# A hybrid decoder step on one core: TensorE's order up to the first FFN pair written out as a table, with planner constants moved

## The chip, the cores and the metric

The kernel runs on one core of one Trainium2 chip. The metric is the device time of one execution in microseconds (us). Engines are named as in the profile: PE is TensorE, DVE is VectorE, ACT is ScalarE, POOL is GpSimd, SP is SyncE (here it only issues DMAs).

## The reference, cut to what matters

One layer for 2048 prompt tokens and 8 single-token samples, width 1024, all in float32:

```python
xn = _rmsnorm(x, norm1_g)
z = jnp.einsum('btd,de->bte', xn, w_in)
xr, gr, q, k, v = jnp.split(z, IN_SPLITS, axis=-1)
xc, new_conv = _causal_conv(xr, conv_buf, conv_w, conv_b)
hs, h_last = _rglru(xc, h0, gate_a_w, gate_a_b, gate_x_w, gate_x_b, lru_lambda)
rec = hs * jax.nn.gelu(gr)
att = sliding-window attention over self + 128 tokens, 8 heads on 2 KV heads, sinks
mix = jnp.concatenate([_rmsnorm(rec, rec_norm_g), _rmsnorm(att, attn_norm_g)], axis=-1)
h = x + jnp.einsum('bte,ed->btd', mix, w_out)
hn = _rmsnorm(h, norm2_g)
ff = jax.nn.silu(hn @ w_gate) * (hn @ w_up)
y = h + ff @ w_down
```

followed by a final RMSNorm. The FFN is 2816 wide.

## The kernel before, in words

Activations lie with channels on the 128 partitions and tokens along the free axis. A float32 product is made of three fp32r matmuls, weight high times input high, high times low, and low times high (`mm3` in the projections, the three calls in `products` and `down` in the FFN).

**The first stage** works on four blocks of tokens (520, then 3 × 512), block `s`. For each: load and norm (`xn{s}_{k}`, k of 8 channel chunks), the input projection in 14 column units (`ip{s}_{u}_{i}`, PSUM tiles of 260 or 512 tokens), convolution (`xc`), the two gates (`g{s}_{c}_{gi}`: one small matmul each, ACT's tanh to `ra` and `ia`), the scan, and attention in 16 blocks of 128 tokens: scores `s{b}_{kv}`, exponentials `sc`, four transposes `pt{b}_{kv}_{kb}`, ACT's `pth` and DVE's `ptl` (high and low part), output `o{b}_{kv}` and its scale `ratt`. Mean squares go through PE too: `st_*` sums over partitions, DVE and POOL turn the sum into 1/root (`cols`), `bc_*` spreads it over the partitions, and ACT copies it to a tile `rb_*`. The output projection `op{s}_{m}` has 8 units `m`. The last block's (`out_half`) is cut into halves: `op3_m_0` over the recurrent channels is added to the residual at once; `op3_m_1` over the attention channels is multiplied on DVE by `rb_at3` (L941), which comes from `bc_at3_0`, and then added to `xres3_m` (L942), which ACT's queue stores to `hs`.

**The FFN** runs over three groups of tokens of two halves each (344 or 342), and over 11 pairs of 128-wide chunks of the 2816. In a pair, 2 × 2 blocks are multiplied with seven products, in the order 1, 2, 6, 5, 7, 3, 4 (`g{group}_{pair}_{r}` for gate, `u...` for up, 12 matmuls each), with sums of weights `s1` to `s4` made on POOL, high parts of weights `w_g.._r` cast on ACT and low parts made on DVE or POOL. Product 1 is copied out of PSUM by ACT to `c_g0_0_10` (L1236) before product 6 continues in the same bank. The inputs of the products are tiles `hn0_*`: four loads `m0_r_kk` for each of seven mixed inputs from DRAM, through four staging tiles, each split into a high part on ACT (L432) and a low part on DVE (L433). The down products are `d{group}_{pair}_{m}_{half}` (tile names `pd`).

**What sets the order.** Each piece of work is a generator; the class `Chains` keeps them in a heap by due time, and a generator yields the time at which its next part is due, from constants: `T_IP` and `T_OP` for the projections of the four blocks, `T_OPA` for the second halves of the last output projection, `T_B0` for the start of the FFN, `F_HN` for the leads of the `hn` loads, `T_ATT`, `T_REC`, `D_ATT` and `D_REC` for attention and recurrence, and leads `L_*` by which single operations go ahead. The due time becomes the priority of what is emitted, and a list scheduler puts each engine's instructions in order by priority and by what is ready in its own model of time. PSUM is eight banks: three for projections and products (`acc_tile`), two for scores, one each for transposes, for attention outputs and for the small tiles (`m_tile`: gates, `st`, `bc`, `hb`, `vt`).

Of the kernel before, what the change touches and what calls it, by code (L numbers as in the profile page):

```python
# [12 lines left out]
P = 128  # L13
# [42 lines left out]
F_HN = [26.25, 18.3, 31.9]  # L56
# [44 lines left out]
T_B, T_END, T_PROD, T_DOWN, T_ROUND = plan()  # L101
O_KF = [8, 9, 10, 11, 12, 13, 0, 4, 1, 5, 2, 6, 3, 7]
# [6 lines left out]
T_REC = 46.56  # L109
L_PE, L_EV, L_DMA, L_W, L_PREP, D_PREP, L_AN, T_HN, D_HN, D_MIX = 195.07, 6.8, 44.07, 6.54, 16.82, -0.58, 33.49, 477.25, 7.78, 0.2  # L110
# [3 lines left out]
L_SW = 10.68  # L114
T_CACHE, T_LD, T_PRO = 126.26, 3.73, -37.62
D_REC = [10.95, 7.47]
D_ATT = [4.5, 3.07, 9.75, 5.73]
T_DVE = -4.47
T_DEC = 102.0
T_RN = [128.93, 254.29, 363.658, 427.88]  # L120
# [70 lines left out]
def hybrid_step(tc, xT, xR, vecs, cst, gatew, win, wout, wgate, wup, wdown, kT, vC, ck, cv, sconv, sh0,  # L191
# [4 lines left out]
    with ExitStack() as ctx:  # L196
# [81 lines left out]
        def mm3(out, ws, k, xh, xl, first, last):  # L278
# [3 lines left out]
            nc.tensor.matmul(out, wh, xl, start=False, stop=False)  # L282
            nc.tensor.matmul(out, wl, xh, start=False, stop=last)  # L283
# [16 lines left out]
        def rstd_cols(acc, w, nt, which, out, name, lead=None, pin=False):  # L300
            ps = m_tile(f"st_{name}")
            with ahead(lead):
                for j in range(nt):
                    r = nc.tensor.matmul(ps[:w, j:j + 1], acc[:, j * w:(j + 1) * w], avg[:, which:which + 1],
                                         start=True, stop=True)
                    if pin and j == 0:
                        keep(r)
            nc.vector.tensor_scalar(out, ps[:w, :nt], EPS, None, ALU.add)
            nc.gpsimd.tensor_tensor(out, out, nhalf[:w, :nt], op=ALU.pow)

        def row_bcast(cols, w, nt, name, lead=None, keep_ps=False, pin=False):
            out = None if keep_ps else bcp.tile([P, TM], F32, tag="bc", name=f"rb_{name}")
            per = 512 // w
            for j0 in range(0, nt, per):
                jn = min(per, nt - j0)
                ps = (acc_tile if keep_ps else m_tile)(f"bc_{name}_{j0}")
                with ahead(lead):
                    for j in range(jn):
                        r = nc.tensor.matmul(ps[:, j * w:(j + 1) * w], cols[:, j0 + j:j0 + j + 1].to_broadcast([w, P]),
                                             ident[:w, :w], start=True, stop=True)  # L320
# [4 lines left out]
                nc.scalar.copy(out[:, j0 * w:(j0 + jn) * w], ps[:, :jn * w])  # L325
            return out
# [7 lines left out]
        def half_bcast(gi, n, name):  # L334
# [3 lines left out]
            for s, (c0, T, _, w, nt) in enumerate(SUBS):  # L338
# [4 lines left out]
                with ahead():  # L343
                    for j in range(j0, j1):
                        x, y = max(a, c0 + j * w), min(b, c0 + j * w + w)
                        d0 = x - c0 - j * w
                        nc.tensor.matmul(ps[:, x - o:y - o], rs2[:w, s, j:j + 1].to_broadcast([w, P]),
                                         ident[:w, d0:d0 + y - x], start=True, stop=True)
# [91 lines left out]
        with ExitStack() as actx:  # L440
# [114 lines left out]
            def unit(s, u, dst, key=None):  # L555
# [7 lines left out]
                for i, (n0, nn) in enumerate(nbl):  # L563
                    ps = (first_tiles.pop(0) if first_tiles else acc_tile)(f"ip{s}_{u}_{i}")
                    for k in range(KD):
                        mm3(ps[:, :nn], w, k, xn[k][:, 0, n0:n0 + nn], xn[k][:, 1, n0:n0 + nn], k == 0, k == KD - 1)
# [10 lines left out]
            def rec_chunk(s, c):  # L577
# [26 lines left out]
                for gi, (dst, hb) in enumerate(((ra, hab), (ia, hxb))):  # L604
                    for n0, nn in nbl:
                        ps = m_tile(f"g{s}_{c}_{gi}_{n0}")
                        with ahead():
                            nc.tensor.matmul(ps[:, :nn], gw[:, (gi * 4 + c) * P:(gi * 4 + c + 1) * P], xc[:, n0:n0 + nn],
# [104 lines left out]
            def v_chunk(s):  # L713
                vr = ap2.tile([P, TM], F32, tag="xres", name=f"vraw{s}")
                yield from unit(s, 9, vr, ("k", s))
                for b in range(4):
                    yield ip_time(s, 9) + U_IP + b
                    ps = m_tile(f"vt{s}_{b}")
                    with ahead():
                        nc.tensor.transpose(ps[:, 0:P], vr[:, b * P:(b + 1) * P], ident)  # L720
# [19 lines left out]
            def attn_item(s, b, kv, t):  # L740
# [19 lines left out]
                for g2 in range(2):  # L760
                    ps = s_tile(f"s{gb}_{kv}_{g2}")
                    for gi in range(2):
# [21 lines left out]
                for i, kb in enumerate(kbs):  # L784
                    yield t + D_ATT[2] + i
                    pt = t_tile(f"pt{gb}_{kv}_{kb}")
                    with ahead():
                        for g in range(G):
                            nc.tensor.transpose(pt[:, g * P:(g + 1) * P], sc[:, g, i * P:(i + 1) * P], ident)
# [7 lines left out]
                for i, (kb, ph, pl) in enumerate(pts):  # L797
                    vt = vts[gb - 1 + kb][:, 2 * kv:2 * kv + 2, :].rearrange("p a d -> p (a d)")
                    with ahead():
                        nc.tensor.matmul(po, vt, ph, start=i == 0, stop=False)  # L800
                        nc.tensor.matmul(po, vt, pl, start=False, stop=i == len(pts) - 1)
# [6 lines left out]
            def decode(t):  # L808
# [17 lines left out]
                for b in range(NB):  # L826
                    nc.tensor.matmul(ps[:, b * 8:b * 8 + 8], kc[:, b * P:(b + 1) * P], qf[:, b * 8:b * 8 + 8],
# [7 lines left out]
                nc.tensor.transpose(ps2[0:64, 0:P], st, ident)  # L835
                nc.tensor.matmul(ps2[0:64, P:P + 1], w1[:, 128:192], ones[:, 0:1],
# [17 lines left out]
                nc.tensor.transpose(ps3[:, 0:64], sd[:, 0:P], ident[0:64, 0:64])  # L854
                nc.tensor.matmul(ps3[:, 64:128], ones[0:64, :], dg, start=True, stop=True)
# [3 lines left out]
                for b in range(NB):  # L859
                    nc.tensor.matmul(ps4[:, b * 8:b * 8 + 8], vc[:, b * P:(b + 1) * P], pt[:, b * 8:b * 8 + 8],  # L860
# [10 lines left out]
                nc.tensor.transpose(ps5[0:NB, 0:P], kvn[:, 0, :], ident)  # L871
                nc.tensor.transpose(ps5[0:NB, P:2 * P], kvn[:, 1, :], ident)
# [6 lines left out]
            def out_unit(s, m):  # L879
# [27 lines left out]
            def out_half(s, m, i):  # L907
# [75 lines left out]
        with ExitStack() as bctx:  # L983
# [181 lines left out]
            def products(gi, p, x):  # L1165
# [52 lines left out]
                for i, r in enumerate(PRODS):  # L1218
# [7 lines left out]
                    for kk in range(4):  # L1226
# [4 lines left out]
                        nc.tensor.matmul(ps, wh, hi, start=first, stop=False, skip_group_check=not fresh)  # L1231
                        nc.tensor.matmul(ps, wh, lo, start=False, stop=False, skip_group_check=not fresh)  # L1232
                        nc.tensor.matmul(ps, wl, hi, start=False, stop=kk == 3, skip_group_check=not fresh)  # L1233
# [20 lines left out]
            def down(gi, p):  # L1254
# [6 lines left out]
                for i, (m, n) in enumerate(order):  # L1261
                    yield t + U_D * i / 16, ("d", gi, p, 0, m // 4), ("d", gi, p, 1, m // 4)
                    ps = ps_tile(f"pd{gi}_{p}_{m}_{n}")[:, :nn]
                    for h in range(2):
# [3 lines left out]
                        nc.tensor.matmul(ps, w[:, 0, c:c + P], hi, start=h == 0, stop=False)  # L1268
                        nc.tensor.matmul(ps, w[:, 0, c:c + P], lo, start=False, stop=False)  # L1269
                        nc.tensor.matmul(ps, w[:, 1, c:c + P], hi, start=False, stop=h == 1)  # L1270
# [8 lines left out]
            def down_parts(gi, p):  # L1279
                nn = HALVES[gi][0][1]  # L1280
                acc = {}
                for n in range(14):
# [6 lines left out]
                    for j in range(2):  # L1289
# [73 lines left out]
            ch.run()  # L1363

# [100 lines left out]
```

## Time and profile before

| what | value |
|---|---|
| median of 3 runs | 2086.74 us (2085.59 to 2092.28) |
| profiled execution | 2083.33 us |
| its span, first to last instruction | 2081.6 us |
| mean granted PE clock | 0.988 |
| PE busy | 2020.7 us, 97% |
| first matmul | 8.10 us |
| start of the FFN's third product (`g0_0_6`) | 697.81 us |

The profile is of one execution. In a timeline row stand start, duration, engine, line of the kernel, operation, output and inputs by name without numbers, and how many equal instructions the row holds; in brackets the idle time ahead of it and what ended that. A row of a stretch gives its limits, its length, the busy time of PE, PEld (weight loads), DVE, ACT and POOL with the number of instructions, PE's granted clock, the DMA engines' busy share and GB/s.

### The profile page before, as it was taken

What the parts mean: (1) busy time and instruction counts of PE and PEld (TensorE: products, weight loads), DVE (VectorE), ACT (ScalarE), POOL (GpSimd) and SP (SyncE); (2) the same over time, 40 slices, a digit from 0 to 9 for tenths busy, and PEclk for the clock granted to TensorE, in tenths of its full rate; (3) what the DMA queues carried; (4) which work ended last, traced back from release to release, by engine and by line L of the source; (5) the groups of instructions that cost most, each with busy time, mean ns of one, the idle gap of its engine ahead of it and who ended that gap; (6) DMA issues with size and microseconds to landing.
All of it is one profiled execution on the core that took longest, in us unless ns stands there. A gap on an engine that the chain in (4) does not pass through costs nothing.

```text
span 2081.6 us, 34706 instructions
## 1 busy us (share of the span) xinstructions
PE 2020.7 (97%) x12238; PEld 1910.1 (92%) x12238; DVE 1438.9 (69%) x2683; ACT 937.7 (45%) x1954; POOL 935.7 (45%) x820
## 2 busy tenths in 40 slices
PE   8999899999999899999999999999999999999997
PEld 8988787878877799999999999999999999999997
DVE  6786885766986655656654568777776667777676
ACT  5774684553564453334334533333334533333342
POOL 5211342030123688767775845445546622332332
PEclk9999999999999899999999999999999999999998
DMA  8764485575677855556555776767677675556652
GB/s 299 258 212 155 156 290 172 186 239 191 212 265 267 290 215 195 213 194 226 197 188 178 269 263 203 246 232 236 204 249 252 235 232 197 195 189 195 196 181 94
DMA packets 208989, 450.95 MB, mean 217 GB/s; under 512 B 25232, under 2 KB 82720, under 8 KB 208800
## 3 DMA queue, kind: packets, MB, share of 16 engines
q1 hardware_dynamic: 205616, 446.24, 62.8%
q10 hardware_dynamic: 3200, 2.51, 0.4%
q8 instruction: 96, 1.57, 0.3%
q14 instruction: 77, 0.63, 0.1%
HBM read 335.89 MB, written 113.84 MB: 216 GB/s over the span
## 4 chain that ended last, share of the span: by engine, by line
PE 51%; DMA 4%; DVE 4%; POOL 3%; issue 3%; ACT 1%; SPq 0%; DVEq 0%; POOLq 0%; ACTq 0%
PE ps_u L1231 6%; PE ps_u L1232 6%; PE ps_u L1233 6%; PE ps_g L1231 5%; PE ps_g L1232 5%; PE ps_g L1233 5%; PE pw L1296 3%; PE pw L1295 3%; PE pw L1297 3%; PE pd L1268 3%; PE pd L1269 3%; PE pd L1270 3%; DMA n<-hs 2%; DVE y L1323 1%; DMA rd<-in_wdown 1%
## 5 line engine op out<-in xcount | busy, mean ns | idle before, releaser
L1231 PE MATMUL ps_g<-hn,w_g 128*128 128x342 f32 (+1 forms) x924 | 296.6, 321 | 5.5 <-DVE xres L942 2.6
L1231 PE MATMUL ps_u<-hn,w_u 128*128 128x342 f32 (+1 forms) x924 | 297.0, 321 | 1.4 <-ACT c_u L1241 0.8
L1232 PE MATMUL ps_g<-hn,w_g 128*128 128x342 f32 (+1 forms) x924 | 296.0, 320 | 2.4 <-DVE hn L433 2.4
L1232 PE MATMUL ps_u<-hn,w_u 128*128 128x342 f32 (+1 forms) x924 | 296.5, 321 | 0.0
L1233 PE MATMUL ps_g<-hn,w_g 128*128 128x342 f32 (+1 forms) x924 | 295.7, 320 | 0.0
L1233 PE MATMUL ps_u<-hn,w_u 128*128 128x342 f32 (+1 forms) x924 | 294.3, 320 | 0.0
L1301 DVE TENSOR_TENSOR y<-y,pw 128x342 f32<-128x342 f32 x504 | 238.7, 503 | 54.8 <-PE pw L1297 53.9
L281 PE MATMUL ip<-xn,w_in 128*128 128x512 f32 (+1 forms) x560 | 201.2, 364 | 8.1 <-ACT xn L286 8.1
L282 PE MATMUL ip<-xn,w_in 128*128 128x512 f32 (+1 forms) x560 | 201.8, 362 | 0.5 <-DVE xn L287 0.5
L283 PE MATMUL ip<-xn,w_in 128*128 128x512 f32 (+1 forms) x560 | 199.7, 358 | 0.0
L1231 PEld LDWEIGHTS ps_g<-hn,w_g 128*128 128x128 f32 x924 | 174.6, 189 | 7.0 <-DVE xres L942 3.0
L1231 PEld LDWEIGHTS ps_u<-hn,w_u 128*128 128x128 f32 x924 | 175.4, 190 | 2.3 <-ACT c_u L1241 1.1
L1232 PEld LDWEIGHTS ps_g<-hn,w_g 128*128 128x128 f32 x924 | 174.8, 189 | 2.7 <-DVE hn L433 2.7
L1232 PEld LDWEIGHTS ps_u<-hn,w_u 128*128 128x128 f32 x924 | 175.4, 190 | 0.0
L1233 PEld LDWEIGHTS ps_u<-hn,w_u 128*128 128x128 f32 x924 | 174.9, 190 | 0.0
L1233 PEld LDWEIGHTS ps_g<-hn,w_g 128*128 128x128 f32 x924 | 174.7, 189 | 0.0
L1272 DVE TENSOR_TENSOR y<-y,pd 128x344 f32<-128x344 f32 (+1 forms) x240 | 116.8, 506 | 75.0 <-PE pd L1270 73.4
L1197 POOL TENSOR_TENSOR c_u<-c_u,c_g 128x342 f32<-128x342 f32 (+1 forms) x60 | 63.6, 1059 | 209.4 <-DVE c_u L1215 206.3
L1269 PE MATMUL pd<-fl,w_d 128*128 128x344 f32 (+1 forms) x480 | 153.7, 320 | 0.2 <-DVE fl L1186 0.2
L1268 PE MATMUL pd<-fh,w_d 128*128 128x344 f32 (+1 forms) x480 | 151.9, 320 | 1.1 <-DVE y L1272 1.1
L1270 PE MATMUL pd<-fh,w_d 128*128 128x344 f32 (+1 forms) x480 | 152.6, 319 | 0.0
L1186 DVE TENSOR_TENSOR fl<-c_u,fh 128x342 fp32r<-128x342 f32 (+1 forms) x132 | 114.0, 870 | 54.4 <-ACT fh L1185 53.0
(308 smaller groups left out, 5299.4 us busy)
## 6 DMA issues: line engine op xcount, KB each, us to landing
w_g<-split_g SPq DMA_DIRECT2D x88, 512.0 KB, 4.3
w_u<-split_u SPq DMA_DIRECT2D x88, 512.0 KB, 5.0
w_in<-split_w SPq DMA_DIRECT2D x84, 512.0 KB, 3.3
rg<-in_wgate SPq DMA_DIRECT2D x110, 256.0 KB, 3.0
ru<-in_wup SPq DMA_DIRECT2D x110, 256.0 KB, 3.1
w_out<-split_w SPq DMA_DIRECT2D x48, 512.0 KB, 4.5
split_g<-w_g SPq DMA_DIRECT2D x44, 512.0 KB, 3.0
split_u<-w_u SPq DMA_DIRECT2D x44, 512.0 KB, 3.8
```

What stands on the lines that cost most here:

```text
L281: nc.tensor.matmul(out, wh, xh, start=first, stop=False)
L282: nc.tensor.matmul(out, wh, xl, start=False, stop=False)
L283: nc.tensor.matmul(out, wl, xh, start=False, stop=last)
L1186: nc.vector.tensor_tensor(lo, v, hi.bitcast(F32), ALU.subtract)
L1231: nc.tensor.matmul(ps, wh, hi, start=first, stop=False, skip_group_check=not fresh)
L1232: nc.tensor.matmul(ps, wh, lo, start=False, stop=False, skip_group_check=not fresh)
L1233: nc.tensor.matmul(ps, wl, hi, start=False, stop=kk == 3, skip_group_check=not fresh)
L1268: nc.tensor.matmul(ps, w[:, 0, c:c + P], hi, start=h == 0, stop=False)
L1269: nc.tensor.matmul(ps, w[:, 0, c:c + P], lo, start=False, stop=False)
L1270: nc.tensor.matmul(ps, w[:, 1, c:c + P], hi, start=False, stop=h == 1)
L1272: nc.vector.tensor_tensor(ys[gi, n, m], ys[gi, n, m], ps, ALU.add)
L1301: nc.vector.tensor_tensor(v, v, ps, ALU.add)
```

## The change

First, constants of the planner are moved, some thirty in all. The core of them:

```diff
-T_IP = [19.97, 89.2513, 240.41, 360.55]
-T_OP = [187.9747, 327.9525, 449.0, 499.41]
-T_OPA, L_LM = 524.66, 40.7
-T_B0 = 570.19
+T_IP = [20.91, 89.202, 240.477, 360.579]
+T_OP = [187.438, 328.019, 449.71, 496.79]
+T_OPA, L_LM = 515.63, 44.273
+T_B0 = 559.152
...
-F_HN = [26.25, 18.3, 31.9]
+F_HN = [36.192, 30.259, 29.168]
...
-T_ATT = [[-5.16, 6.82], [94.7626, 9.19], [318.03, 12.77], [454.6511, 8.38]]
+T_ATT = [[-11.877, 6.857], [86.931, 4.752], [306.814, 13.349], [454.558, 12.033]]
...
-L_PE, L_EV, L_DMA, L_W, L_PREP, D_PREP, L_AN, T_HN, D_HN, D_MIX = 195.07, 6.8, 44.07, 6.54, 16.82, -0.58, 33.49, 477.25, 7.78, 0.2
+L_PE, L_EV, L_DMA, L_W, L_PREP, D_PREP, L_AN, T_HN, D_HN, D_MIX = 195.07, 11.274, 42.443, 7.573, 17.909, -9.742, 33.056, 477.538, 6.792, 0.2
...
-T_CACHE, T_LD, T_PRO = 126.26, 3.73, -37.62
+T_CACHE, T_LD, T_PRO = 121.342, -20.409, -33.787
```

Second, a table lists PE's matmuls of the first stage and of the first FFN pair by key and count. Every matmul and transpose is noted under its key when it is emitted, and at the end each is tied behind its neighbour in the table by a dependency that orders the issue and adds no semaphore:

```diff
+PE_ORDER = """
+ip0_1_0 ip0_1_1 ip0_12_0 ip0_12_1 ip0_1_0:2 ip0_1_1:2 ip0_12_0:2 ip0_12_1:2 ip0_1_0 ip0_1_1 ip0_12_0 ip0_12_1
...
+"""
...
+        def mm(key, *args, **kw):
+            r = nc.tensor.matmul(*args, **kw)
+            issued.setdefault(key, []).append(r)
+            return r
...
+        def behind(later, earlier):
+            tc.add_manual_dep(later.ins, earlier.ins.name, no_sync, reason="issue order")
+
+        def order_pe():
+            todo, seq = {k: list(v) for k, v in issued.items()}, []
+            for run in PE_ORDER.split():
+                key, _, n = run.partition(":")
+                for _ in range(int(n or 1)):
+                    seq.append(todo[key].pop(0))
+            for a, b in zip(seq, seq[1:]):
+                behind(b, a)
...
-            nc.tensor.matmul(out, wh, xh, start=first, stop=False)
+            mm(key, out, wh, xh, start=first, stop=False)
...
             ch.run()
+            order_pe()
```

Neither part adds or removes a matmul, a vector operation or a DMA. On PE 1310 of 12011 instructions stand at another place, by at most 46 places, the last of them about 800 us into the execution; on DVE 414 are moved, on ACT 249, on SP 80 and on POOL 55. In the changed program the matmuls carry the line of the helper (L358).

The first place is PE at the last output projection, where `st_at3` and `bc_at3_0` stand among the units `op3_m_1`. A row holds equal instructions together; before, each of the three matmuls of a product has a line of its own. Of before, the two surroundings:

```order
L283 MATMUL op3_1_1_6957<-mix3_7_6915,w_out3_1_1_1_6872 128x512
L304 MATMUL st_at3_6925<-avg_105,atacc3_6901 128x1 x4
L281 MATMUL op3_2_1_6975<-mix3_4_6903,w_out3_2_1_1_6874 128x512
...
L283 MATMUL op3_3_1_6993<-mix3_7_6915,w_out3_3_1_1_6952 128x512
L319 MATMUL bc_at3_0_6933<-cs_101,atcols3_6924 128x128 x4
L281 MATMUL op3_4_1_7011<-mix3_4_6903,w_out3_4_1_1_6970 128x512
```

Of the changed program:

```order
L358 MATMUL op3_0_1_6949<-mix3_7_6920,w_out3_0_1_1_6637 128x512
L358 MATMUL st_at3_6935<-avg_105,atacc3_6923 128x1 x4
L358 MATMUL op3_1_1_6965<-mix3_5_6914,w_out3_1_1_1_6641 128x512 x3
L358 MATMUL op3_0_1_6949<-mix3_7_6920,w_out3_0_1_1_6637 128x512 x2
...
L358 MATMUL op3_3_1_6997<-mix3_4_6911,w_out3_3_1_1_6692 128x512 x3
L358 MATMUL op3_3_1_6997<-mix3_5_6914,w_out3_3_1_1_6692 128x512 x3
L358 MATMUL op3_3_1_6997<-mix3_6_6917,w_out3_3_1_1_6692 128x512 x3
L358 MATMUL op3_3_1_6997<-mix3_7_6920,w_out3_3_1_1_6692 128x512
L358 MATMUL bc_at3_0_6943<-cs_101,atcols3_6934 128x128 x4
```

The units now come in the order 3, 2, 4, 6, 5, 7 after 0 and 1; ahead of `bc_at3_0` stand 34 matmuls of these units instead of 48, and ahead of `st_at3` 13 instead of 23.

The second place is ACT a little later, around the copy of the FFN's first product, `c_g0_0_10`, on which PE's product 6 waits. DMA rows here are stores of the residual sums, `hn` casts are the high parts of FFN inputs. Of before:

```order
L432 CAST hn0_1_4_7674<-m0_7_3_7678 128x344
L349 COPY hb_1_1_7936<-hb_1_1_7937 128x342
L1029 CAST w_u0_0_1_7790<-ru0_0_00_7726 128x512
L943 DMA hs_111<-xres3_4_6773 128x512
L1236 COPY c_g0_0_10_7107<-ps_g0_0_1_7758 128x344
L1029 CAST w_u0_0_2_7806<-ru0_0_01_7728 128x512
L432 CAST hn0_1_5_7679<-m0_3_0_7683 128x344
```

Of the changed program:

```order
L533 CAST hn0_1_5_7671<-m0_3_0_7675 128x344
L1044 DMA hs_111<-xres3_6_6818 128x512
L533 CAST hn0_1_6_7680<-m0_3_1_7679 128x344
L1044 DMA hs_111<-xres3_4_6787 128x512
L1130 CAST w_u0_0_1_7790<-ru0_0_00_7726 128x512
L533 CAST hn0_1_6_7680<-m0_3_2_7684 128x344
L1337 COPY c_g0_0_10_7107<-ps_g0_0_1_7758 128x344
```

Three more `hn` casts (`m0_3_0` to `m0_3_2`) and the store of the sum of `op3_6` now stand ahead of the copy; the store of `xres3_4`'s second half, the sum of `op3_5`, stood ahead of it before and still does, with two casts between them now, a weight cast and one of `hn`.

The third place is SP in the same stretch, the loads `m0_3_*` of the FFN inputs among weight loads (`rg`, `ru`) and stores (`split_g`, `y0`). Of before, then of the changed program:

```order
L431 DMA m0_3_1_7687<-mixed_112 128x344
L431 DMA m0_3_2_7692<-mixed_112 128x344
L1082 DMA split_g_113<-w_g0_0_6_7738 128x1024
L1041 DMA rg0_1_10_7827<-in_wgate 128x512
L1082 DMA split_g_113<-w_g0_0_5_7742 128x1024
L1082 DMA split_g_113<-w_g0_0_3_7754 128x1024
L431 DMA m0_3_3_7697<-mixed_112 128x344
```

```order
L532 DMA m0_3_1_7679<-mixed_112 128x344
L1142 DMA rg0_1_00_7823<-in_wgate 128x512
L532 DMA m0_3_2_7684<-mixed_112 128x344
L532 DMA m0_3_3_7689<-mixed_112 128x344
L1183 DMA split_g_113<-w_g0_0_3_7754 128x1024
L1183 DMA split_g_113<-w_g0_0_6_7738 128x1024
```

`m0_3_3` moved ahead of three stores and one weight load.

More of the change, by code (lines that the diff above doesn't have):

```diff
@@ new lines @@
+g0_0_6:12 g0_0_5:12 u0_0_1:12 g0_0_7:12 g0_0_3:12 g0_0_4:4 u0_0_6:12 g0_0_4:2 u0_0_2:9 g0_0_4 u0_0_2:3 g0_0_4:5
+u0_0_5:12 u0_0_7:12 g0_1_1:12 u0_0_3:12 u0_0_4:12 g0_1_6:12 g0_1_2:12 g0_1_5:12 d0_0_0_0:6 d0_0_0_1:6 d0_0_1_0:3
+g0_1_7:12 g0_1_3:12 d0_0_1_0:3 d0_0_1_1:6 d0_0_2_0:3 g0_1_4:12 d0_0_2_0:3 d0_0_2_1:6 d0_0_3_0:6 d0_0_3_1:6
+d0_0_4_0:6 d0_0_4_1:6 u0_1_1:2 d0_0_5_0:6 d0_0_5_1:6 d0_0_6_0:6 u0_1_1 d0_0_6_1:6 d0_0_7_0:6 d0_0_7_1:6 u0_1_1:9
+u0_1_2:12 u0_1_5:12 u0_1_6:12 u0_1_7:12 u0_1_3:12 u0_1_4:12
@@ L303, in rstd_cols @@
                 for j in range(nt):
-                    r = nc.tensor.matmul(ps[:w, j:j + 1], acc[:, j * w:(j + 1) * w], avg[:, which:which + 1],
+                    r = mm(f"st_{name}", ps[:w, j:j + 1], acc[:, j * w:(j + 1) * w], avg[:, which:which + 1],
                                          start=True, stop=True)
```

152 lines of the change are left out of this document (113 added, 39 removed).

## Prediction

> **What bounds the kernel now.** I first read the page's busy shares, then the busy time of each engine in stretches of the program, then the list of what PE waits for, and last the rows around the longest waits.
>
> ```profile
> PE 2020.7 (97%) x12238; PEld 1910.1 (92%) x12238; DVE 1438.9 (69%) x2683; ACT 937.7 (45%) x1954; POOL 935.7 (45%) x820
> ...
> 8.10:200.00 191.90, 188.28 (x1224) 170.92 (x1225) 146.75 (x353) 117.30 (x265) 54.67 (x63) 0.98 0.68 235
> 200.00:300.00 100.00, 89.01 (x569) 77.96 (x568) 82.56 (x158) 69.94 (x148) 41.71 (x35) 0.95 0.60 209
> 300.00:650.00 350.00, 341.58 (x1653) 275.05 (x1652) 259.24 (x551) 190.90 (x398) 73.24 (x82) 0.99 0.64 213
> 650.00:725.00 75.00, 67.64 (x322) 58.90 (x321) 47.81 (x63) 29.45 (x58) 38.13 (x26) 0.91 0.86 304
> 725.00:2081.60 1356.60, 1334.22 (x8479) 1327.21 (x8477) 902.35 (x1557) 526.03 (x1081) 722.87 (x606) 1.00 0.62 211
> ```
>
> The stretches give length, then busy time of PE, PEld, DVE, ACT and POOL, granted clock, DMA share and GB/s. PE is the bound, so only its idle time and its clock can be won without removing work. The change removes none and touches nothing after the first FFN pair, so the last stretch should stay. In the first four, idle time is 3.6 + 11.0 + 8.4 + 7.4 = 30.4 us. To that come the times of low clock: 1 − clock, doubled, times the length is the time at half speed (7.7 + 10.0 + 7.0 + 13.5, 38 us by these rounded clocks).
>
> What low clock costs, and when it comes, stands in four stretches of 3.41 us and four matmuls:
>
> ```profile
> 613.06:616.47 3.41, 1.77 (x8) 1.12 (x8) 2.83 (x11) 3.36 (x6) 1.42 (x2) 1.00 0.96 314
> 616.47:619.90 3.43, 3.43 (x23) 2.99 (x22) 3.43 (x6) 3.42 (x10) 0.09 (x1) 1.00 0.87 310
> 694.98:698.39 3.41, 1.63 (x11) 1.36 (x10) 3.41 (x4) 2.31 (x6) 3.20 (x3) 1.00 0.94 308
> 698.39:701.81 3.42, 2.76 (x10) 2.32 (x9) 3.42 (x5) 1.24 (x3) 3.34 (x3) 0.50 1.00 335
> ...
> 694.94 0.32 PE L1231 MATMUL ps_g<-hn,w_g 128*128 128x344 f32 x1
> 695.10 0.32 PE L1232 MATMUL ps_g<-hn,w_g 128*128 128x344 f32 x1
> ...
> 698.65 0.49 PE L1232 MATMUL ps_g<-hn,w_g 128*128 128x344 f32 x1
> 698.94 0.49 PE L1233 MATMUL ps_g<-hn,w_g 128*128 128x344 f32 x1
> ```
>
> A stretch with 1.64 us of idle PE is followed by full clock; one with 1.78 is followed by 3.42 us at 0.50. A matmul starts 0.16 us after the one before at full clock and 0.29 at half, so such a stretch, filled with work, loses 3.41 × (1 − 0.16/0.29) = 1.5 us. An idle wait past about half a stretch therefore costs its own length and 1.5 us more.
>
> The Trainium skill ("TensorE: Matmul & The Clock Gate", Part 1) has the clock halve after a whole idle window of about 3.4 us; by that, none of the waits here except the start would cost clock, and only idle time could be won. The two rows at 694.98 and 698.39 speak against it: there about half a window of idle time was enough.
>
> **The change part by part.** It fixes PE's order by a table and moves some thirty planner constants, which reorder the other engines a little. The same instructions stand in both programs, so the price is only in waits.
>
> *The boundary from out-projection to FFN* is the largest term.
>
> ```profile
> 664.64 3.11 POOL L298 TENSOR_TENSOR atacc<-atacc,sq_at 128x512 f32<-128x512 f32 x2 [0.31 <-ACT sq_at L297]
> 671.82 0.94 PE L304 MATMUL st_at<-avg,atacc 128*128 128x1 f32 x8
> 673.05 1.02 POOL L309 TENSOR_TENSOR atcols<-atcols,nhalf 128x4 f32<-128x4 f32 x1 [5.30 <-DVE atcols L308]
> 678.28 0.39 PE L283 MATMUL op<-mix,w_out 128*128 128x512 f32 x1
> 678.51 1.05 PE L319 MATMUL bc_at<-cs,atcols 128*128 128x128 f32 x8
> 679.60 0.59 ACT L325 COPY rb_at<-bc_at 128x512 f32<-128x512 f32 x1 [0.27 <-PE bc_at L319]
> 680.22 2.50 DVE L941 TENSOR_TENSOR op<-op,rb_at 128x512 f32<-128x512 f32 x4 [7.25 <-ACT rb_at L325]
> ...
> 697.31 0.45 ACT L1236 COPY c_g<-ps_g 128x344 f32<-128x344 f32 x1
> 697.81 0.42 PE L1231 MATMUL ps_g<-hn,w_g 128*128 128x344 f32 x1 [1.78 <-ACT c_g L1236]
> 703.00 0.67 DVE L942 TENSOR_TENSOR xres<-xres,op 128x512 f32<-128x512 f32 x1
> 703.73 0.43 PE L1231 MATMUL ps_g<-hn,w_g 128*128 128x344 f32 x1 [2.58 <-DVE xres L942]
> 713.57 1.57 DVE L433 TENSOR_TENSOR hn<-m,hn 128x344 fp32r<-128x344 f32 x1
> 715.19 0.44 PE L1232 MATMUL ps_g<-hn,w_g 128*128 128x344 f32 x1 [2.40 <-DVE hn L433]
> 716.52 0.66 PE L1231 MATMUL ps_u<-hn,w_u 128*128 128x344 f32 x1 [0.60 <-DVE c_g L1215]
> ...
> 690.00:716.00 26.00, 19.16 (x98) 17.48 (x97) 20.30 (x25) 11.87 (x24) 17.23 (x12) 0.86 1.00 364
> ```
>
> PE loses 1.78 + 2.58 + 2.40 + 0.60 = 7.36 us here, and four stretches run at half clock (one after each of the first two waits, two after the last pair), 4 × 1.5 = 6.0 us: 13.4 in all. Behind the first two stands one DVE chain, which starts when the broadcast `bc_at3_0` is copied and runs without a gap to 705. After the change 34 matmuls of `op3_*_1` stand ahead of that broadcast instead of 48; at 0.23 us each (678.28 to 678.51) it comes 14 × 0.23 = 3.2 us earlier, at 675.3. What it needs allows that: `st_at3` moves ten places, to 669.5, when POOL's sum has been ready since 667.75; POOL's power ended 2.25 us after `st_at3` started, so now at 671.7. DVE was idle for 7.25 us, so its chain starts at 677.0.
>
> In the new DVE order the sum of `op3_7` has the same number of steps ahead, one of them an `hn` product in place of a weight difference (0.3 longer): 703.00 − 3.2 + 0.3 = 700.1. The bank of `g0_0_5` is then free before PE comes to it, and that wait goes. But the COPY that lets `g0_0_6` start stands on ACT behind the store of the sum of `op3_5`, as before, and now behind three casts of `hn` more. That sum has four more DVE steps ahead than before and, counted with 0.6 (scale, sum), 0.95 (`hn`), 1.4 (weights) from 677.0, ends at about 697.7; store issue 0.33, three casts and the copy put `g0_0_6` at about 699.2, 1.4 later than now. So the first wait grows to 3.2 us and keeps its slow stretch. `m0_3_3`, the load behind the 2.40 us, is moved ahead of three stores and a weight load on SP and ahead of the first gate sum on DVE; it should be multiplied by 704, and PE wants it at about 708: both last waits go. Left are 3.2 us idle and one slow stretch: 13.4 − 4.7 = **−8.7 us**. Ends: if the ACT copy waits for a late load, −4 or nothing; if it doesn't wait at all, −13.4.
>
> *Other places.*
>
> ```profile
> 107.88 1.24 PE L608 MATMUL g<-xc,gw 128*128 128x260 f32 x2 [1.05 <-ACT ra L610]
> 109.13 0.42 PE L282 MATMUL ip<-xn,w_in 128*128 128x260 f32 x1
> ...
> 441.06 0.47 PE L800 MATMUL o<-pth,vt 128*128 128x512 f32 x1 [1.91 <-DVE ratt L805]
> ...
> 253.38 0.66 PE L789 MATMUL pt<-cs,sc 128*128 128x128 f32 x4 [1.64 <-DVE ptl L793]
> 270.60 1.12 PE L608 MATMUL g<-xc,gw 128*128 128x512 f32 x2 [3.84 <-ACT ra L610]
> 286.90 1.12 PE L608 MATMUL g<-xc,gw 128*128 128x512 f32 x2 [0.94 <-DVE xc L595]
> 8.08 0.96 DVE L287 SCALAR_TENSOR_TENSOR xn<-xs,vec,xn 128x520 fp32r<-128x520 f32 x1 [7.02 <-ACT xn L286]
> ```
>
> At 107.88 six matmuls of 0.12 us move ahead of `g0_3_0_260`: 0.7 of its 1.05 us is filled, and the slow stretch behind it (0.42 us a matmul) probably goes: between −0.7 and −2.5, I take −2.0. At 441.06 a load of a row tile goes ahead of a 512 KB weight load on SP, and its ACT step ahead of a square; the wait may shrink by all or nothing, and with it a slow stretch: 0 to −3.4, taken −1.0. At 286.90 DVE makes `xc1_3` earlier: −0.8.
>
> Against these, `pt5_0_1` (253.38) and `g1_2_1_0` (270.60) are put 6 and 8 matmuls earlier, though their inputs come no sooner on DVE, and on ACT a copy and a square now stand ahead of the gate: 0.7 and 1.0 us more wait. The 3.84 us behind the first absorb what PE loses there, unless the wait passes half a stretch: between 0 and +4.7, taken +0.8. Between 75 and 91 us a dozen small steps come six matmuls earlier with little slack: 0 to +2, taken +0.4. At the start DVE has some 18 tiny steps put ahead of the first `xn`; it was idle for 7.02 us there, so 0 to +2, taken +0.3.
>
> The sum is −8.7 − 2.0 − 1.0 − 0.8 + 0.8 + 0.4 + 0.3 = **−11 us** on an execution of 2083.33 us (span 2081.6 and 1.7 around it), to 2072.3. The median of the three runs is 2086.74, 3.4 above that execution; I put the difference on the median: **2075.7**, in round numbers 2076.
>
> **The rivals.**
>
> *The boundary gives nothing.* DMA runs at a share of 1.00 from 690 to 716. If the loads of `hn` land no earlier than now, ACT's copy, queued behind two of their casts, waits with them, to 702: 6 us of idle PE and two slow stretches instead of the 7.36 and four. The boundary then gives 4.4, which the costs of the other places may eat: 2083 to 2087. For it speaks the full DMA; against it that on SP these loads are issued past only a few others.
>
> *The first pair is short of weights, and the kernel slower.*
>
> ```profile
> 711.48 3.28 POOL L1064 TENSOR_TENSOR s_g<-rg,rg 128x512 f32<-128x512 f32 x2
> 731.08 1.31 POOL L1030 TENSOR_TENSOR w_g<-rg,w_g 128x512 fp32r<-128x512 f32 x1 [1.11 <-ACT w_g L1029]
> 732.43 0.32 PE L1231 MATMUL ps_g<-hn,w_g 128*128 128x344 f32 x1
> ```
>
> The low half of `w_g0_1_1` is ready at 732.39, and PE uses it at 732.43. The table puts this product ahead of 24 others, 3.8 us earlier, and with the gain above PE wants it at 720. POOL's new order does bring it forward by one step, but eight steps of about 1.5 us remain from 711.48: 723 if POOL never waits, 728 with the 5 us of waits that it has now. If POOL starts no earlier than today, PE waits 8 us and two or three slow stretches follow: +12 on −11. If the waits add up as they do now until 732, it is +16: 2091. It decides from about 731 on. Against it: POOL's start depends on a cast that waits for PE, so it moves forward with PE.
>
> *The table has no effect of note*, since the waits are set by chains on ACT and DVE which keep their pace: 2085 to 2088. Against it stands the broadcast, which is late by PE's order alone.
>
> **How the numbers follow.** A measurement of this kernel tells about 0.3% (6.3 us) from no change, so faster means under 2080.5 and slower over 2093. My sum holds with its near variants at 0.60 (2066 to 2080); the boundary that gives nothing, or little, 0.20; weights short, with the early small steps all at their upper ends, 0.15 (2084 to 2097); no effect 0.05. Half of the slow case stays inside 2091. So the range is 2066 to 2091, and faster 0.60, same 0.27, slower 0.13.
>
> **What would show it.** Right: the broadcast at about 675.5, DVE's chain from 677, no wait of `g0_0_5`, `g0_0_3` and `u0_0_2`, one slow stretch instead of four, and PE ahead of before by 8 to 9 us at the end of the first pair's gate. Wrong: `g0_0_6` waiting beyond 701, or a wait of over 2 us at `g0_1_1`; or new waits of over 1.7 us at `pt5_0_1` and `g1_2_1_0` with a half clock behind. A start of PE later than 8.1 would be a loss that nothing later gives back.

## The result and the profile after

The change makes no difference that can be measured. Over 20 runs of each, the changed kernel takes 2084.48 us (median, 2078.05 to 2091.44) and the kernel before 2084.26 (2078.01 to 2092.28); the ratio is 1.000 with a 95% interval of 0.9987 to 1.0013, that is ±2.7 us. The 2084.48 us lie inside the forecast's range of 2066 to 2091, but its likeliest case, 2076 us and so 11 us faster, did not come.

The profiled execution of the changed kernel took 2078.05 us, span 2076.3. It is the fastest of the twenty, so its 5.3 us less than the profile of before say nothing about the two kernels: runs of one order differ by 13 to 14 us. What the profiles can tell is where in the program time is won and lost. Of the changed kernel, the busy shares and the stretches shown of before:

```profile
PE 2014.0 (97%) x12238; PEld 1903.0 (92%) x12238; DVE 1440.0 (69%) x2683; ACT 939.9 (45%) x1954; POOL 929.3 (45%) x820
...
8.10:200.00 191.90, 187.14 (x1225) 169.16 (x1226) 142.03 (x344) 118.09 (x265) 52.37 (x61) 1.00 0.70 235
200.00:300.00 100.00, 88.76 (x580) 77.25 (x579) 85.27 (x160) 72.47 (x151) 42.03 (x36) 0.98 0.62 212
300.00:650.00 350.00, 341.01 (x1645) 274.74 (x1644) 257.63 (x548) 189.74 (x396) 67.76 (x81) 0.99 0.66 213
650.00:725.00 75.00, 71.39 (x373) 63.16 (x372) 49.68 (x66) 34.62 (x69) 43.00 (x31) 0.98 0.94 333
725.00:2076.30 1351.30, 1325.72 (x8423) 1318.70 (x8421) 901.58 (x1552) 520.85 (x1069) 719.02 (x601) 1.00 0.63 210
```

Only the fourth stretch, the boundary, changed much: PE busy 71.39 us of 75 instead of 67.64, clock 0.98 instead of 0.91. In the first three, idle time is 4.8 + 11.2 + 9.0 us; it was 3.6 + 11.0 + 8.4. Row by row, the boundary went as forecast. Of the changed kernel, PE, ACT, DVE and POOL there:

```profile
668.54 0.95 PE L358 MATMUL st_at<-avg,atacc 128*128 128x1 f32 x8
674.29 1.05 PE L358 MATMUL bc_at<-cs,atcols 128*128 128x128 f32 x8
675.38 0.59 ACT L426 COPY rb_at<-bc_at 128x512 f32<-128x512 f32 x1 [9.79 <-PE bc_at L358]
676.00 1.89 DVE L1042 TENSOR_TENSOR op<-op,rb_at 128x512 f32<-128x512 f32 x3 [6.32 <-ACT rb_at L426]
...
697.03 0.44 ACT L1337 COPY c_g<-ps_g 128x344 f32<-128x344 f32 x1
697.52 4.80 PE L358 MATMUL ps_g<-hn,w_g 128*128 128x344 f32 x19 [2.45 <-ACT c_g L1337]
697.97 0.69 DVE L1043 TENSOR_TENSOR xres<-xres,op 128x512 f32<-128x512 f32 x1
718.50 1.57 POOL L1131 TENSOR_TENSOR w_g<-rg,w_g 128x512 fp32r<-128x512 f32 x1
720.13 1.07 PE L358 MATMUL ps_g<-hn,w_g 128*128 128x344 f32 x5 [1.03 <-POOL w_g L1131]
...
690.00:716.00 26.00, 23.42 (x134) 22.39 (x133) 21.30 (x27) 13.73 (x30) 18.28 (x14) 0.93 0.96 351
```

PE came to the boundary 1.0 us earlier, so the forecast's 675.3 for the broadcast is 674.3 here, and its 677.0 for DVE's chain is 676.0: both are met. At 734 us, where both orders have issued the same matmuls, PE was 8.7 us ahead of before (8 to 9 forecast), 7.7 of them won at the boundary. The waits of `g0_0_5`, `g0_0_3` and `u0_0_2` are gone; the one of `g0_0_6` grew from 1.78 to 2.45 (3.2 forecast). A new one of 1.03 us stands at `g0_1_1`, where POOL's weight difference ends at 720.07. From 690 to 716, PE ran 134 matmuls instead of 98, with one slow stretch (3.41 us at half clock) instead of four.

### The profile page after: what moved, and what is told of

It is laid out like the page before. It is cut to its first block, busy times and chain, and to the rows that moved or that the text cites. A ratio compares the mean times of both kernels' runs of the same rounds, so it can differ in the third digit from the quotient of the medians.

```text
span 2076.3 us, 34690 instructions
## 1 busy us (share of the span) xinstructions
PE 2014.0 (97%) x12238; PEld 1903.0 (92%) x12238; DVE 1440.0 (69%) x2683; ACT 939.9 (45%) x1954; POOL 929.3 (45%) x820
## 4 chain that ended last, share of the span: by engine, by line
PE 69%; DVE 12%; DMA 9%; issue 4%; ACT 3%; POOL 2%; SPq 1%; DVEq 0%; ACTq 0%; POOLq 0%
PE ps_u L358 17%; PE ps_g L358 17%; PE pd L358 10%; PE ip L358 10%; PE pw L358 9%; DMA n<-hs 4%; PE op L358 2%; DMA rd<-in_wdown 1%; DMA xs<-in_xT 1%; DMA mixed<-n 1%; DVE y L1424 1%; DVE xc L696 1%; DVE n L485 1%; DVE n L477 1%; PE o L358 1%
## 5 line engine op out<-in xcount | busy, mean ns | idle before, releaser
L358 PE MATMUL ps_g<-hn,w_g 128*128 128x342 f32 (+1 forms) x2772 | 491.9, 321 | 4.7 <-ACT c_g L1337 2.5
L358 PE MATMUL ps_u<-hn,w_u 128*128 128x342 f32 (+1 forms) x2772 | 482.5, 320 | 0.7 <-ACT c_u L1342 0.7
L358 PEld LDWEIGHTS ps_g<-hn,w_g 128*128 128x128 f32 x2772 | 447.0, 189 | 6.4 <-ACT c_g L1337 2.7
L358 PEld LDWEIGHTS ps_u<-hn,w_u 128*128 128x128 f32 x2772 | 444.3, 189 | 1.6 <-ACT c_u L1342 1.0
L358 PE MATMUL ip<-xn,w_in 128*128 128x512 f32 (+1 forms) x1680 | 354.3, 360 | 11.7 <-ACT xn L387 8.3
L358 PEld LDWEIGHTS ip<-xn,w_in 128*128 128x128 f32 x1680 | 274.2, 192 | 57.1 <-ACT xn L387 8.3
L358 PE MATMUL pd<-fh,w_d 128*128 128x344 f32 (+1 forms) x960 | 238.7, 321 | 1.5 <-DVE y L1373 1.5
L358 PE MATMUL op<-mix,w_out 128*128 128x512 f32 (+1 forms) x960 | 205.1, 359 | 1.5 <-ACT mix L777 1.4
L358 PEld LDWEIGHTS op<-mix,w_out 128*128 128x128 f32 x960 | 156.2, 189 | 30.5 <-issue 5.3
L358 PE MATMUL pw<-fh,wd 128*128 128x342 f32 x576 | 168.2, 321 | 2.5 <-DVE y L1402 2.5
L358 PEld LDWEIGHTS pd<-fh,w_d 128*128 128x128 f32 x960 | 168.2, 188 | 2.1 <-DVE y L1373 1.8
L358 PE MATMUL pd<-fl,w_d 128*128 128x344 f32 (+1 forms) x480 | 154.0, 321 | 1.6 <-DVE fl L1287 1.6
L358 PE MATMUL pw<-t,wd 128*128 128x342 f32 x648 | 125.1, 320 | 3.7 <-DVE y L1402 3.7
L358 PEld LDWEIGHTS pw<-t,wd 128*128 128x128 f32 x648 | 105.8, 189 | 5.3 <-DVE y L1402 4.9
```

The source lines that it names most:

```text
L358: r = nc.tensor.matmul(*args, **kw)
```

## The experiments

Time is too coarse for terms of one to three us, so the kernels that follow were also read by a common clock: the start of the matmul at five places of PE's order, at which the old and the new order have issued the same work. The places are 1228 (about 210 us), 1957 (350), 3353 (`op3_0_1`, 666), 3644 (`g0_1_2` in the old order, `g0_1_6` in the new, 734), 4207 (`pd0_2_0_1`, 823), with the first matmul ahead and the last one of the program behind. Fourteen profiles of fourteen executions give for each part the time in the old and in the new order:

| part, us | old order: mean (s.d., profiles) | new order: mean (s.d., profiles) | new − old |
|---|---|---|---|
| first matmul to 210 | 200.4 (2.2, 7) | 202.5 (1.1, 6) | +2.2 ± 1.0 |
| 210 to 350 | 139.5 (0.5, 7) | 139.4 (0.8, 7) | −0.1 ± 0.4 |
| 350 to 666 | 314.7 (2.8, 7) | 313.6 (1.5, 7) | −1.1 ± 1.2 |
| boundary, 666 to 734 | 66.9 (1.4, 8) | 61.0 (1.1, 6) | −5.9 ± 0.7 |
| 734 to 823, by order of the boundary | 89.6 (0.6, 8) | 91.0 (0.7, 6) | +1.5 ± 0.4 |
| 823 to the end, by order of the boundary | 1249.1 (2.2, 8) | 1250.3 (2.0, 6) | +1.2 ± 1.1 |

The ± is one standard error. The first row takes the new order with either start, and leaves out the run of the start alone. The profiles are of several chips. On each of the three that have both orders the new boundary is the shorter one, by 7.6, 4.6 and 4.8 us.

The kernels made for these runs have PE's order tied by a table; old and new pieces are joined at places where both have issued the same matmuls. Times were taken in three sets, each on one chip with 35 runs of the kernel before beside it; the medians of before are 2078.78, 2081.47 and 2081.59 us. Each ratio is to before on the same chip; it is the ratio on record and can differ a little from that of the two medians. Differences in us are worked out from the ratio.

**The boundary alone**, with the old order and the old constants ahead of it:

```diff
-T_IP = [20.91, 89.202, 240.477, 360.579]
+T_IP = [19.97, 89.2513, 240.41, 360.55]
...
 T_OPA, L_LM = 515.63, 44.273
 T_B0 = 559.152
...
 F_HN = [36.192, 30.259, 29.168]
...
-ip0_1_0:2 ip0_1_1:2 ip0_12_0:2 ip0_12_1:5 ip0_9_0:3 st_x0:5 ip0_9_0:21 ip0_9_1:18 bc_x0_0:4 ip0_9_1:6 ip0_8_0:24
+ip0_1_1:2 ip0_12_0:2 ip0_12_1:5 ip0_9_0:3 st_x0:5 ip0_9_0:21 ip0_9_1:18 bc_x0_0:4 ip0_9_1:6 ip0_8_0:19 bc_x0_4 ip0_8_0:5
```

> PE's order, and that of every other engine, is the old one through the first stage and the new one from the first op3_m_1 on. Theory A (the boundary really gains about 7 us, as the pair of profiles shows between 646 and 734 us, and the first stage gives it back in the usual run): 7 us faster than before, ratio about 0.9965. Theory B (the waits of the boundary vary from run to run, or the gain is given back further on in the FFN): within 2 us of before. Theory C (the old first stage hands over its work in such a state that the new boundary waits more): same or slower, with a wait of over 3 us at g0_0_6.

Measured: 2077.1 against 2078.78 us, ratio 0.9988 (0.9975 to 1.0002). It was run a second time, as an exact copy:

> The new boundary alone once more, to halve the interval of the first run of it (0.9975 to 1.0002). From the profiles by part -6.2 + 2.8 = 3.4 us faster (0.9984). In the profile: no wait at g0_0_5 and g0_0_3, 60 to 63 us from op3_0_1 to g0_1_2 instead of 66 to 69, and 1338 to 1343 us from there to the last product instead of 1335 to 1340. If the boundary has no gain in the usual run: 1.000 within 0.001, and with it these figures as in the old order.

Measured: 0.9998 (0.9982 to 1.0013). The boundary took 62.7 and 61.9 us in the two profiles, the parts behind it 1341.9 and 1342.4. So the gain is there in the profile and smaller in the time: theory A's 7 us fall, and of theory B the half that has the gain given back further on is in part supported (see below). Theory C has something too; of this kernel, PE's longest wait there, in both profiles:

```profile
693.53 3.81 PE L356 MATMUL ps_g<-hn,w_g 128*128 128x344 f32 x12 [4.75 <-ACT c_g L1335]
```

```profile
694.59 5.98 PE L356 MATMUL ps_g<-hn,w_g 128*128 128x344 f32 x24 [4.75 <-ACT c_g L1335]
```

The first wait is 4.75 us here and 1.3 to 2.9 in the four other profiles with the new boundary. ACT's rows ahead of it, of the first run, show what the copy stands behind:

```profile
689.77 0.62 ACT L1128 CAST w_u<-ru 128x512 fp32r<-128x512 f32 x1 [2.39 <-DVE xres L1041]
690.29 0.47 ACT L531 CAST hn<-m 128x344 fp32r<-128x344 f32 x1
691.91 0.33 ACTq L1042 DMA_DIRECT2D hs<-xres  x1
692.28 0.86 ACT L531 CAST hn<-m 128x344 fp32r<-128x344 f32 x2 [1.51 <-DVE xres L1041]
693.04 0.44 ACT L1335 COPY c_g<-ps_g 128x344 f32<-128x344 f32 x1
```

A cast, a store that waits for DVE's sum, and two casts of `hn`: the queue of the forecast.

**The first stage alone**, with the old boundary:

```diff
-T_OPA, L_LM = 515.63, 44.273
-T_B0 = 559.152
+T_OPA, L_LM = 524.66, 40.7
+T_B0 = 570.19
...
-F_HN = [36.192, 30.259, 29.168]
+F_HN = [26.25, 18.3, 31.9]
```

and the table's part from the first `op3_0_1` on in the old order.

> The new order through the first stage, the old one from the first op3_m_1 on. Theory A (the first stage loses about 7 us in the usual run): 5 to 8 us slower than before, ratio about 1.003. Theory B: within 2 us of before, with op3_0_1 starting at the same time as before within 2 us.

Measured: 2084.71 us, ratio 1.0027 (1.0015 to 1.0039), 5.6 us slower. The loss of theory A is there. Its profile shows the old boundary's waits again:

```profile
695.62 3.28 PE L359 MATMUL ps_g<-hn,w_g 128*128 128x344 f32 x12 [2.18 <-ACT c_g L1338]
701.73 3.81 PE L359 MATMUL ps_g<-hn,w_g 128*128 128x344 f32 x12 [2.83 <-DVE xres L1044]
713.79 0.94 PE L359 MATMUL ps_g<-hn,w_g 128*128 128x344 f32 x2 [2.40 <-DVE hn L535]
715.34 3.81 PE L359 MATMUL ps_u<-hn,w_u 128*128 128x344 f32 x12 [0.60 <-DVE c_g L1317]
```

**Both kernels once more**, for the spread:

> The changed kernel once more, for a second profile of the same order. Theory A: the same boundary (idle 3 to 4 us from 690 to 716, no half clock or one stretch of it), and a first stage that is some us longer than in the first profile, which was of the fastest run. Theory B: a boundary that differs by several us from that of the first profile. Ratio 1.000 within 0.002.

Measured: 1.0002 (0.9989 to 1.0014); boundary 59.7 us, after 60.1 in the first profile, with 3.4 us idle from 690 to 716 and full clock there. Theory A's other half failed: PE came to `op3_0_1` at 662.9 us, 2.7 earlier than in the first profile and not later. This profile too is of the fastest of its twelve runs, so it doesn't show the usual first stage.

> The kernel before once more: ratio 1.000 within 0.002, and a second profile that says how far the waits of the first stage and of the boundary differ from run to run. Theory A: the boundary shows again 7 us idle and about four slow stretches; theory B: it differs by several us.

Measured: 1.0005 (0.9992 to 1.0018); boundary 68.9 us, after 67.8. The boundary's length repeats, but not all waits of the first stage do. Of the second profile of before, the rows that answer to 23.73, 270.60 and 441.06:

```profile
22.58 1.08 PE L304 MATMUL st_x<-avg,xacc 128*104 128x1 f32 x10
265.17 1.54 PE L608 MATMUL g<-xc,gw 128*128 128x512 f32 x2 [2.07 <-ACT ra L610]
433.01 0.47 PE L800 MATMUL o<-pth,vt 128*128 128x512 f32 x1 [0.23 <-DVE ratt L805]
442.44 0.39 PE L767 MATMUL s<-KK,qst 128*128 128x256 f32 x1 [0.94 <-DVE mx L771]
```

The wait at `st_x0`, 1.58 us in the first profile, is absent; 3.84 us at `g1_2_1_0` are 2.07; 1.91 us at `o9_0` are 0.23, with a new 0.94 a little later. PE came to `op3_0_1` 7.1 us earlier than in the first profile, with the same program.

**The first stage in three parts**, the old constants everywhere, the new table only up to place 1228, from there to 1957, or from there to 3353. The edit of the first (the others are of the same kind):

```diff
-T_OP = [187.438, 328.019, 449.71, 496.79]
+T_OP = [187.9747, 327.9525, 449.0, 499.41]
...
-op0_0_260:2 op0_1_0:2 o4_1_0:2 op0_1_260:4 o4_1_1:2 op0_1_260:20 op0_2_0:11 pt5_0_1:4 op0_2_0:12 o5_0_0:2 op0_2_0
+op0_1_0:3 g1_1_1_0 op0_0_0:2 op0_0_260:2 op0_1_0:2 o4_1_0:2 o4_1_1:2 op0_1_260:24 op0_2_0:17 pt5_0_1:4 op0_2_0:3 o5_0_0:2
```

> PE's new order only as far as 210 us (PE place 1228), the old one behind it, the old constants. The first stage as a whole cost 5.6 us in the run of it alone. Theory A (the loss is in the beginning: waits of about 1 us at 111 and 126 that the old order didn't have): 3 to 5 us slower than before. Theory D (the loss is spread over all parts): 1 to 2 us slower. Theory E (the loss is in the last part, where three new waits of 1 to 1.7 us stand at bc_at2, g3_2_1_0 and op3_0_0): no change.

> PE's new order only from 210 to 350 us. New waits: o5_0 1.05, pt5_1_1 1.67, 0.8 more at pt5_0_1; gone: 1 to 2 us at g1_2_1_0 and 0.9 at g1_3_0_0. Theory A and E: no change within 2 us; theory D: 1 to 2 us slower.

> PE's new order only from 350 to 666 us. Theory E: 4 to 6 us slower than before. Theory A: no change within 2 us. Theory D: 1 to 2 us slower.

Measured: 1.0002 (0.9992 to 1.0012), 0.9997 (0.9984 to 1.0011) and 0.9999 (0.9986 to 1.0013). None shows the loss: theories A and E fall, and D isn't told from nothing, since 1 us is within each interval.

**The table without the constants.**

```diff
-T_CACHE, T_LD, T_PRO = 121.342, -20.409, -33.787
+T_CACHE, T_LD, T_PRO = 126.26, 3.73, -37.62
```

and all other constants likewise, the table as in the changed kernel.

> The whole table with all the old constants; PE's order is that of the changed kernel, and of the other engines 55 DVE, 37 ACT, 10 POOL and 7 SP instructions stand elsewhere than in the changed kernel, most of them in the first 10 us, where DVE no longer has its small steps ahead of the first xn. If the constants matter by that start alone, its profile lacks the second wait of about 1.4 us at 11 us and it is 1 to 2 us faster than the changed kernel, so 0 to 2 faster than before. If the table is the whole change: ratio 1.000 within 0.0015 and the same waits as in the changed kernel from 100 us on.

Measured: 0.9995 (0.9980 to 1.0011). Its profile has the waits of the changed kernel at 111 (1.06), 126 (1.01), 261 (1.07), 275 (1.66) and 638 us (1.25), and a boundary of 61.2 us; only the start is the old one, with 1.68 us at `st_x0` and no second wait. So by its waits the table is nearly the whole change; the interval of the time is too wide to tell more.

**The start alone** is the edit above the other way round, on the old order:

```diff
-T_CACHE, T_LD, T_PRO = 126.26, 3.73, -37.62
+T_CACHE, T_LD, T_PRO = 121.342, -20.409, -33.787
```

> PE's old order and old constants everywhere, but the new start: DVE's small preparing steps ahead of the first xn. Theory F (the start is what the first stage loses: the run of the new first stage was 5.6 us slower, its three parts with the old start 0.4, -0.6 and -0.2): 3 to 5 us slower than before. Theory G (the start trades a wait of 1.6 us at st_x0 with a slow stretch, which old starts have in some executions, for one of 1.4 us at 11 us in every execution): within 1.5 us of before, st_x0 without a wait.

Measured: 1.0002 (0.9989 to 1.0016). PE reaches `st_x0` without a wait there, but at 25.1 us; the four profiles with the new start have 24.7 to 25.1, the ten with the old one 22.6 to 24.0. Of the start alone:

```profile
8.51 1.24 PE L356 MATMUL ip<-xn,w_in 128*128 128x260 f32 x4 [8.51 <-ACT xn L385]
10.90 1.45 PE L356 MATMUL ip<-xn,w_in 128*128 128x260 f32 x5 [1.16 <-DVE xn L386]
25.09 0.99 PE L356 MATMUL st_x<-avg,xacc 128*104 128x1 f32 x10
```

**The new first stage with the old start:**

```diff
-T_OPA, L_LM = 515.63, 44.273
+T_OPA, L_LM = 524.66, 40.7
...
-T_CACHE, T_LD, T_PRO = 121.342, -20.409, -33.787
+T_CACHE, T_LD, T_PRO = 126.26, 3.73, -37.62
```

> The new order of the first stage with the old constants and so the old start, and the old boundary. Theory F: no change, within 2 us of before. Theory G and the rival that the parts of the first stage cost only together: 3 to 6 us slower, as the run of the new first stage was.

Measured: 1.0021 (1.0005 to 1.0037), 4.4 us slower. This speaks against theory F: the loss is there without the new start.

**The old order to 210 us, the new one behind it**, for a version that beats both:

```diff
-T_ATT = [[-11.877, 6.857], [86.931, 4.752], [306.814, 13.349], [454.558, 12.033]]
+T_ATT = [[-5.16, 6.82], [94.7626, 9.19], [318.03, 12.77], [454.6511, 8.38]]
...
-ip0_8_1:4 bc_x0_4 ip0_8_1:20 ip0_0_0:24 ip0_0_1:19 g0_1_0_0 ip0_0_1:5 ip0_3_0:20 g0_1_0_260 ip0_3_0:4 ip0_3_1:12
+ip0_8_1:24 ip0_0_0:24 ip0_0_1:10 g0_1_0_0 ip0_0_1:14 ip0_3_0:11 g0_1_0_260 ip0_3_0:13 ip0_3_1:12 g0_1_1_0 ip0_3_1:12 ip0_11_0:13
```

> The old order and start up to 210 us, the new order from there on, the boundary with it. From the profiles by part: -6.2 at the boundary, -0.8 from 210 to 666 us, +2.8 in the rest of the FFN, together 4 us faster than before (ratio 0.998). If the gain of the boundary is wholly given back behind it: no change.

Measured: 1.0003 (0.9985 to 1.0021). No gain; the boundary took 60.5 us in its profile, the parts behind it 1343.7.

## Why the forecast missed, point by point

**The sum by time.** The four combinations of first stage and boundary give, with the mean of like runs: old and old 1; new first stage, old boundary 1.0024; old first stage, new boundary 0.9993; both new 0.9999 (the changed kernel twice and the table without constants). The new boundary is worth 0.0007 and 0.0025 in the two pairs, in the mean 0.0016 or 3.3 us; the new first stage costs 0.0024 and 0.0006, in the mean 0.0015 or 3.1 us. With intervals of ±0.0013 on each run these are worth about ±1.6 us. The forecast had −8.7 and −2.3 for them. So two steps failed: the boundary's yield, and the terms of the first stage, whose sum had the wrong sign. That the time still fell into the range is luck: 2084 is where the rival "the boundary gives nothing" put it (2083 to 2087), but the boundary did give, and something else took it.

**The boundary: the mechanism was right, its yield too large.** Broadcast, chain and the three vanished waits came where the working put them, and the ACT queue ahead of the copy did lengthen the first wait in the profile of the changed kernel, as it said. Over six profiles against eight the boundary is 5.9 us shorter, not 8.7. Most of the difference is in the slow stretches. The forecast took the four of one profile and left one, which is 3 × 1.5 = 4.5 us; the eight profiles with the old boundary have 4, 4, 5, 2, 2, 2, 2 and 2, the six with the new one 0 to 2, in the mean 2.9 and 1.3, and at 1.5 us each that is 2.3 us. Idle time fell by 3.5 us in the mean, from 8.0 to 4.5; the forecast had 4.2. In those 4.5 stand the first wait, which is anything from 1.3 to 4.75 us, and about one us at `g0_1_1` in four of the six; the second profile of the changed kernel has 1.83 at `u0_0_1` besides. `g0_1_1` is the place of the second rival: PE came at 719 and POOL's difference ended at 720.07, so the rival had the right queue and a tenth of its price.

The price of a slow stretch is not fully understood either. In the first profile of before, the stretch from 637.00 to 640.36 has only 0.53 us of idle PE (3.36 − 2.83), and the next, to 643.80, runs at 0.50 all the same. So half a stretch of idle time is not the whole rule; what sets this one is open.

Then 1.5 ± 0.4 us are given back before 823: in the changed kernel PE waits 1.24 us there, against 0.17 in the first profile of before:

```profile
815.84 0.43 PE L358 MATMUL pd<-fl,w_d 128*128 128x344 f32 x1 [1.24 <-DVE fl L1287]
```

That wait is 1.24 to 2.34 us in all six profiles with the new boundary; three of the eight with the old one have about 1.25 us there, the others 0.2 or less. So "the last stretch should stay" failed too: some of what PE gains at the boundary it waits for on DVE later. The 1.2 ± 1.1 us behind 823, where the order is the same, are not shown to be a loss: on two of the three chips that have both boundaries the difference there is within 0.3 us. The profiles then give −5.9 + 1.5 = −4.4 us for the new boundary, which agrees with the 3.3 ± 1.6 of the times.

**The terms of the first stage failed as a sum.** At 107.88 the wait fell to 0.31, and PE's lead over the first profile of before grew from 0.7 to 3.5 us by 110, somewhat more than forecast (2.0). But part of that was a draw: the wait is in all eight profiles with the old order there (0.84 to 1.06), the slow stretch behind it in two. And two new waits followed behind DVE's `rrec`, which the forecast didn't have; by 135 us the lead was 0.1:

```profile
111.40 0.96 PE L358 MATMUL ip<-xn,w_in 128*128 128x512 f32 x3 [0.79 <-DVE rrec L673]
126.49 0.51 PE L358 MATMUL ip<-xn,w_in 128*128 128x260 f32 x2 [1.02 <-DVE rrec L673]
```

These projections wait for a PSUM bank, whose reader on DVE (L673) comes later than PE; both waits are in all six profiles with the new order there (0.69 to 1.10 and 1.01 to 1.02). The forecast looked only at waits that the old order had. From 210 to 350 the terms were −0.8 and +0.8, and the measured sum is −0.1 ± 0.4. Of the changed kernel, the rows that answer to 253.38 and 270.60, and the new wait behind them:

```profile
252.55 0.66 PE L363 MATMUL pt<-cs,sc 128*128 128x128 f32 x4 [2.36 <-DVE ptl L894]
260.93 0.50 PE L358 MATMUL o<-ptl,vt 128*128 128x512 f32 x1 [1.05 <-DVE ptl L894]
268.24 0.70 PE L358 MATMUL g<-xc,gw 128*128 128x512 f32 x1 [1.31 <-ACT ra L711]
274.63 0.30 PE L363 MATMUL pt<-cs,sc 128*128 128x128 f32 x1 [1.67 <-DVE ptl L894]
```

`pt5_0_1`, put six matmuls ahead, waits 0.72 us longer (0.7 forecast); what that cost came off the wait of `g1_2_1_0`, and 0.94 at `g1_3_0_0` went while 1.67 at `pt5_1_1` came. The start was put at +0.3 out of 0 to 2: by `st_x0` it is 1.8 us (24.9 against 23.2 in the mean), near the upper end. By 34 us it is 1.1 in the mean, because four of the ten old starts lose a slow stretch behind `st_x0`.

**The term of 441 us was no term.** That wait, 1.91 us and a slow stretch in the one profile, is 0 to 0.6 in the six other profiles that have the old order there. The forecast took each wait of one execution as a property of the order. Those that repeat are (0.91 or 0.92 at 215 us and 2.57 at 219 in all seven profiles with the old order there, 2.40 to 2.43 at `g0_0_3` in all eight with the old boundary); the others, and above all the slow stretches, differ from execution to execution.

**The level** was off as well: the median of three runs, 2086.74, is 2.5 above that of twenty.

**What stays open.** Which waits make the 3 to 5 us of the first stage: as a whole it is 5.6 and 4.4 us slower with the old boundary, its three parts and the start alone sum to nothing (+0.4, −0.6, −0.2, +0.4), each ±2 to 3 us. Either the parts cost only together, or the small losses hide in the intervals, or the chip matters: the whole was measured on two chips and its three parts on a third. By the profiles the first 210 us are the likeliest place (+2.2 ± 1.0), but half of that is the start; from 34 to 210 us it is +1.1 ± 0.5. Also open is why the new boundary gains less behind the old first stage than behind the new one, if it does (0.0018 less, known to about ±0.0016); the 4.75 us at `g0_0_6` in both of its profiles are a part of that.

## What to carry to other kernels

A wait in one profile is worth a term only if it comes again: take a second profile of the unchanged kernel and count those that repeat, and do the same with slow stretches. When PE's instructions are put elsewhere, look for the new waits with the same care as for the old ones, above all for PSUM banks whose readers keep their pace. A gain in one stage is a loan until the next engine in line has been followed to the end: here 5.9 us at the boundary were about 3 in the time, and an order that cost as much elsewhere took those.

## What the hardware showed

Some small DVE steps are held while POOL works. Of the changed kernel, DVE's preparing steps at the start, and POOL's row at that time:

```profile
4.71 0.16 DVE L590 TENSOR_TENSOR sp<-sp,vec 128x4 f32<-128x4 f32 x1
5.14 1.17 DVE L592 TENSOR_SCALAR sp<-sp 128x4 f32<-128x4 f32 x1
6.55 0.97 DVE L594 TENSOR_TENSOR sp<-sp 128x4 f32<-128x4 f32 x1
7.55 1.20 DVE L595 TENSOR_TENSOR sp<-sp 128x4 f32<-128x4 f32 x1
9.19 0.17 DVE L599 TENSOR_SCALAR sp<-sp 128x4 f32<-128x4 f32 x1
```

```profile
5.02 3.71 POOL L348 TENSOR_TENSOR w_in<-raw_in,w_in 128x512 fp32r<-128x512 f32 x3
```

Steps over 128x4 take 0.15 to 0.18 us elsewhere, but three of the four that lie between 5.0 and 8.73, beside POOL's three differences of 1.24 us each, took 0.97 to 1.20. POOL's three end at about 6.26, 7.50 and 8.73, the held steps at 6.31, 7.52 and 8.75. In the second profile of the changed kernel POOL pauses from 7.19 to 7.40: the step that starts in the pause, at 7.25, takes 0.16 us, and the next, at 7.45, takes 1.25. The hold costs the moved steps about 2.8 us, and DVE's first `xn` starts at 10.09 instead of 8.08; PE's second wait, 1.41 us at 10.90, is for it. The Trainium skill ("SBUF — State Buffer", "Who interferes with whom") says that where DVE and GpSimd both need the port pair that they share, the one that comes second is blocked for the other's whole instruction. The trace agrees: each held step ends within 0.05 us of the end of one of POOL's.

The first 24 us of the old start come in two kinds: four of the ten profiles have a wait of 1.6 to 1.7 us at `st_x0`, the others 0 to 0.25, with PE's order there the same in all. The two profiles of before, which are of one program, are one of each kind.
